# Attention scores of two heads in the two halves of the array's rows, queries and keys as single loads

## The chip, the cores and the metric

The kernel runs on one core of a Trainium2 chip. The metric is device time in microseconds of one execution, the median of several runs. The engines are PE (TensorE, matmuls), DVE (VectorE), ACT (ScalarE), POOL (GpSimd) and SP (SyncE, which issues transfers). Lines such as L745 are lines of the kernel before.

## What is computed

One layer of an encoder over 2048 tokens of width 1024, float32 in and out. The token grid is 32 rows of 64 columns.

```
h = rms_norm(x, norm1_g);  proj = h @ w_in
hy_in, q, k, v, pool_in = split(proj)              # 768, 512, 512, 512, 256 columns
y_hy   = hyena_mixer(hy_in, ...)                   # FFT convolution: irfft(rfft(z) * rfft(filter))
y_na   = neighbourhood_attention(q, k, v, rpb)     # 8 heads of 64; each token sees 8 x 16 neighbours
y_pool = pool_mixer(pool_in, ...)
x = x + concat(rms_norm of each of the three) @ w_out
x = x + expert_choice_moe(rms_norm(x), ...)        # 16 experts, 256 tokens each
out = rms_norm(x, final_g)

neighbourhood_attention, per head:
    s = (q / 8) . k_neighbours + rpb[row offset, column offset];  p = softmax(s);  out = p . v_neighbours
```

## The kernel before

The stages follow each other: `proj` (projections, with the filter's and Hyena's spectra and the pooling between them), `attention`, `out_proj`, `top_tokens`, `experts`. A scheduler that runs at build time sets the order of the instructions on each engine from the program's order and a simulated timeline; semaphores come from the tiles' uses. A tile's tag with `bufs=n` has n buffers, and the n+1st use waits for the first one's readers.

Numbers are carried as a high and a low part in the matmul type float32r. The split of the product is high x high + high x low + low x high, three terms. `mm3` (L219) issues three matmuls for it.

**Projections.** `slab` (L293) makes 128 columns of `proj` for 512 tokens. For queries (s of 3 and 4) it writes the high part to `QHd` from ACT and the low part to `QLd` from POOL (L323 to L325), for keys (s of 5 and 6) the two parts to the two halves of `KD` (L330, L331). On the host, `_layouts` (L154) puts the weight columns of a pair of heads in an order in which the dimensions of the two heads alternate, so that one partition's row of a load holds both heads.

**Filter and Hyena.** `filt` (L339) computes the filter's spectrum in 8 groups of four and writes each with one transfer to `Hd` (L413). Its `mm3` at L390 works on 64-row slices, the forward filter in the upper and the backward one in the lower half of the rows. `hyena` (L423) loads a group of `Hd` from SP (L479), and L490 multiplies it with the spectrum of z by four products of 64 partitions x 512 for each half group.

**Attention.** There are 16 units (hg, rb, g): two groups of four heads, four blocks of 8 grid rows, and g = 0 for the two outer column blocks of 16, g = 1 for the two inner ones. They are numbered 0 to 15 in this order. `load(u)` (L665) and `load_values(u)` are put in the program one unit ahead, at the beginning of unit u - 1. `load` fetches the keys of the row block (at g = 0; two transfers on SP, L680; what the block before already holds is copied by POOL), the queries (three transfers of 64 partitions, L685: the high part into both halves of the tile at_q1, from SP and from POOL, and the low part into the upper half of at_q2, from SP; the lower half of at_q2 was filled with zeros once, L653) and the bias tables (`load_bias`, L626: one tile per column block, reloaded for every row block but the third, parts from slot 4 on from POOL and the others from SP, L638). The value tiles of g = 1 are loaded once per group of heads, 1 MB each from SP (L705).

For each head the keys of high and low part lie one below the other in 128 rows, so L745 gives high x high + high x low and L746 adds low x high. L750 (DVE) adds the bias and takes the minimum, L753 (ACT) the exponential, L758 (PE) transposes it into a bank tp, L762 or L764 (DVE or ACT in turn) copies it out, and for every second head L772 (PE) multiplies with the values into a bank o, the two heads in the two halves of the array's columns. The PSUM banks of this stage are s=3, tp=3, o=2 (L1291). `load_wo` splits the weights of the output projection between the units, and `mix` (L822) prepares the first chunk of `out_proj` near the end of attention; its sums use a bank s.

## Time and profile before

| | |
|---|---|
| median of 3 runs | 3381.33 us (3378.48 to 3384.32) |
| profiled execution | 3379.93 us |
| its span | 3377.7 us |
| mean granted clock of PE | 0.973 |
| PE busy | 3222.4 us, 95% |
| DVE busy | 1919.4 us, 57% |
| ACT busy | 1519.5 us, 45% |
| POOL busy | 375.0 us, 11% |
| moved by DMA | 681.30 MB, mean 202 GB/s |

The span is the time from the first to the last instruction of the profiled execution. Busy shares are means over stages with different limits: the chain of work that ended last, followed back from the last instruction, says what set the end, and the table by stage says where. A granted clock of 1.00 is 2.4 GHz and 0.50 is 1.2 GHz; a stretch with both shows a mean. A PE piece in the chain lasts from its start to the next one's start, so pieces can be added up; the "mean ns of one" of a matmul includes its way through the array and overlaps with its neighbours.

### The profile page before, as it was taken

The page shows a single profiled execution, that of the slowest core. Times are in us where ns is not written, and L with a number is a line of the kernel's source. Part 1 is how long each engine was busy: PE and PEld are TensorE (multiplying, and loading weights), DVE is VectorE, ACT ScalarE, POOL GpSimd, SP SyncE. Part 2 cuts the span into 40 slices and gives each one's busy share as a digit, 9 for nine tenths or more (in the row PEclk, how much of TensorE's full clock was granted, in tenths as well). Part 3 has the DMA queues.
Part 4 walks back from the last instruction along what each step waited for, and adds up shares of the span by engine and source line. Part 5 has one row for each costly group of instructions (what it writes and reads, how often), then busy time and mean ns, then how long its engine had stood idle before and what let it go on. Part 6 is the DMA issues. An engine that isn't in the chain of part 4 may idle for free.

```text
span 3377.7 us, 44794 instructions
## 1 busy us (share of the span) xinstructions
PE 3222.4 (95%) x17874; PEld 2710.8 (80%) x17874; DVE 1919.4 (57%) x2571; ACT 1519.5 (45%) x2004; POOL 375.0 (11%) x492
## 2 busy tenths in 40 slices
PE   8999999687999499999999999999999999999998
PEld 6888897465788388888888888888888888888886
DVE  5124557354677665665656656556566565565665
ACT  4134422254533254554544545445445454454554
POOL 2211212222211000000000000000000000000011
PEclk9999999797999699999999999999999999999999
DMA  6675686877554356576665666666657666566586
GB/s 220 214 247 184 217 279 225 196 184 167 161 168 164 115 187 200 198 205 198 199 204 195 211 199 200 202 199 194 204 192 208 202 197 206 193 212 200 195 296 231
DMA packets 425221, 681.30 MB, mean 202 GB/s; under 512 B 28258, under 2 KB 325970, under 8 KB 424630
## 3 DMA queue, kind: packets, MB, share of 16 engines
q1 hardware_dynamic: 365414, 525.45, 49.1%
q0 software_dynamic: 31728, 111.39, 11.7%
q10 hardware_dynamic: 27872, 41.61, 3.5%
q8 instruction: 140, 2.29, 0.3%
q14 instruction: 67, 0.55, 0.0%
HBM read 573.86 MB, written 114.83 MB: 204 GB/s over the span
## 4 chain that ended last, share of the span: by engine, by line
PE 89%; DMA 7%; issue 2%; DVE 2%; ACT 1%; SPq 0%; POOL 0%; POOLq 0%; DVEq 0%; ACTq 0%
PE mm L1141 27%; PE mm L1143 14%; PE mm L221 13%; PE mm L223 13%; PE mm L222 13%; PE o L772 2%; DMA at_t<-Ce 1%; PE tp L758 1%; DMA at_q<-QLd 1%; PE tp L1110 1%; DMA Bd<-t 1%; DMA mo_xg<-Hr,mo_ix 1%; DMA mx_q<-Rd 1%; PE s L745 1%; DMA at_vw<-Vc 0%
## 5 line engine op out<-in xcount | busy, mean ns | idle before, releaser
L1141 PE MATMUL mm<-mo_xx,mo_wh 128*128 128x512 f32 x4096 | 1443.1, 397 | 0.6 <-DVE mo_xx L217 0.6
L217 DVE TENSOR_TENSOR mo_wl<-mo_raw,mo_wh 128x2048 fp32r<-128x2048 f32 x384 | 879.8, 2291 | 784.3 <-ACT mo_wh L216 784.2
L1143 PE MATMUL mm<-mo_xx,mo_wl 128*128 128x256 f32 x4096 | 1150.8, 281 | 0.0
L216 ACT ACTIVATE mo_wh<-mo_raw 128x2048 fp32r<-128x2048 f32 x384 | 735.3, 1915 | 702.2 <-issue 324.6
L1141 PEld LDWEIGHTS mm<-mo_xx,mo_wh 128*128 128x128 f32 x4096 | 769.6, 188 | 183.7 <-DVE mo_xx L217 1.0
L1143 PEld LDWEIGHTS mm<-mo_xx,mo_wl 128*128 128x128 f32 x4096 | 774.3, 189 | 0.7
L222 PE MATMUL mm<-mo_wl,mo_hh 128*128 128x512 f32 x1024 | 398.5, 389 | 0.0
L221 PE MATMUL mm<-mo_wh,mo_hh 128*128 128x512 f32 x1024 | 398.1, 389 | 0.0
L223 PE MATMUL mm<-mo_wh,mo_hl 128*128 128x512 f32 x1024 | 396.1, 389 | 0.0
L223 PEld LDWEIGHTS mm<-mo_wh,mo_hl 128*128 128x128 f32 x1024 | 192.2, 188 | 40.0
L221 PEld LDWEIGHTS mm<-mo_wh,mo_hh 128*128 128x128 f32 x1024 | 192.2, 188 | 39.9
L222 PEld LDWEIGHTS mm<-mo_wl,mo_hh 128*128 128x128 f32 x1024 | 192.2, 188 | 39.6
L1174 POOL DMA_INDIRECT Acc<-mo_y,mo_ix x30 | 69.0, 2301 | 1392.2 <-ACT mo_y L1173 1275.3
L221 PE MATMUL mm<-hT_h,w_h 128*128 128x512 f32 x512 | 205.3, 403 | 2.1 <-ACT hT_h L216 1.7
L222 PE MATMUL mm<-hT_l,w_h 128*128 128x512 f32 x512 | 207.1, 404 | 0.0
L223 PE MATMUL mm<-hT_h,w_l 128*128 128x512 f32 x512 | 206.3, 403 | 0.0
L1149 ACT ACTIVATE mo_s<-mo_s 128x512 f32<-128x512 f32 x128 | 81.0, 633 | 237.1 <-DVE mo_s L1146 237.1
L1146 DVE TENSOR_TENSOR mo_s<-mo_s,mm 128x512 f32<-128x512 f32 x256 | 174.1, 680 | 0.0
L1145 ACT ACTIVATE mo_s<-mm 128x512 f32<-128x512 f32 x256 | 147.7, 577 | 0.0
L750 DVE CUSTOM_DVE_ANT_1 at_s<-s,at_t 128x360 f32<-128x360 f32 (+5 forms) x128 | 66.9, 537 | 94.5 <-DMA at_t<-Ce 59.4
L221 PEld LDWEIGHTS mm<-hT_h,w_h 128*128 128x128 f32 x512 | 96.9, 190 | 26.1 <-ACT hT_h L216 2.4
L222 PEld LDWEIGHTS mm<-hT_l,w_h 128*128 128x128 f32 x512 | 96.8, 189 | 25.5 <-issue 3.1
(306 smaller groups left out, 3772.2 us busy)
## 6 DMA issues: line engine op xcount, KB each, us to landing
mo_raw<-in_w_gate SPq DMA_DIRECT2D x128, 1024.0 KB
mo_raw<-in_w_up SPq DMA_DIRECT2D x128, 1024.0 KB
mo_raw<-in_w_down SPq DMA_DIRECT2D x128, 1024.0 KB
w_r<-c_w_in_t SPq DMA_DIRECT2D x40, 512.0 KB
x<-in_x SPq DMA_DIRECT2D x16, 512.0 KB
Ud<-e ACTq DMA_DIRECT2D x32, 256.0 KB
wo_x<-in_x SPq DMA_DIRECT2D x16, 512.0 KB
Acc<-wo_x POOLq DMA_DIRECT2D x16, 512.0 KB, 4.2
```

The source lines that it names most:

```text
L216: self.nc.scalar.activation(hi, src, AF.Copy)
L217: self.nc.vector.tensor_tensor(lo, src, hi.bitcast(F), op=OP.subtract)
L221: mm(out, lhsT=lh, rhs=rh, start=start, stop=False)
L222: mm(out, lhsT=lh, rhs=rl, start=False, stop=False)
L223: mm(out, lhsT=ll, rhs=rh, start=False, stop=stop)
L772: nc.tensor.matmul(po[hh % 2 * 64:hh % 2 * 64 + 64, h // 2, :], lhsT=v[0:n * nkc, ci, hh * 64:hh * 64 + 64], rhs=pp[0:n * nkc, ci, :], sta ...
L1141: nc.tensor.matmul(pt[:, m].rearrange("p k t -> p (k t)"), lhsT=w[:, d, ms], rhs=xx[:, d].rearrange("p k t -> p (k t)"), start=d == 0, sto ...
L1143: nc.tensor.matmul(pt[:, m, 1], lhsT=wlo[:, d, ms], rhs=xx[:, d, 0], start=False, stop=d == 7)
L1145: nc.scalar.activation(a, pt[:, :, 1], AF.Copy)
L1146: nc.vector.tensor_tensor(a, a, pt[:, :, 0], op=OP.add)
L1149: nc.scalar.activation(s, s, AF.Silu)
L1174: nc.gpsimd.indirect_dma_start(out=self.Acc, out_offset=off, in_=y, in_offset=None, compute_op=OP.add)
```

## The change

The weight columns of queries and keys are no longer reordered on the host. Queries go to one tensor `QD` in which a partition holds high and low part of all four heads in 4 KB, and are loaded with one transfer over 128 partitions into a tile at_q. Keys go to `KD` with the two parts as columns, and are loaded with one transfer. A partition's rows are those of one head of a pair: the first head in partitions 0 to 63, the second in 64 to 127. For a pair, six matmuls of 64 rows (high x high, low key x high query, high key x low query, for each of the two heads in turn) write to two neighbouring banks of one tile `pair`. The banks become s=2 pairs, tp=2, o=2; the sums of `mix` in attention take a bank o. All tables but those of unit 0 are loaded from SP. The second half of a value tile of g = 1 comes from POOL. In the filter the real and the imaginary part of a group are each written to `Hd` twice, into both halves of the partitions, in four transfers; Hyena loads both tiles, and forms its products with one operation on 128 partitions and two on 64 in place of four on 64.

The diff, without the blank lines and the declarations:

```
@@ -171,11 +171,7 @@
     h[:, 18:24] = a["hy_short_b"][0].reshape(6, 128).T
     h[:, 24:26] = a["hy_skip"][0].reshape(2, 128).T
-    w = a["w_in"][0].reshape(2, 4, 128, 10, 256).copy()
-    qk = w[:, :, :, 3:7].reshape(2, 4, 128, 4, 2, 2, 64)
-    w[:, :, :, 3:7] = qk.swapaxes(5, 6).reshape(2, 4, 128, 4, 256)
-    w = np.ascontiguousarray(w.transpose(3, 0, 2, 1, 4))
+    w = np.ascontiguousarray(a["w_in"][0].reshape(2, 4, 128, 10, 256).transpose(3, 0, 2, 1, 4))
     rpb = a["na_rpb"][0][:, ::-1, ::-1].reshape(2, 4, 15, 31).transpose(0, 2, 1, 3)
     return {"par_f": f, "par_p": g, "par_h": h, "w_in_t": w, "rpb_r": np.ascontiguousarray(rpb).reshape(120, 31)}
@@ -320,15 +316,15 @@
             for k, b in enumerate(self.QB):
                 nc.vector.scalar_tensor_tensor(ql[:, k], pv[:, b], -0.125, qh[:, k].bitcast(F),
                                                op0=OP.mult, op1=OP.subtract)
-            for eng, dst, src in ((nc.scalar, self.QHd, qh), (nc.gpsimd, self.QLd, ql)):
-                eng.dma_start(dst[s - 3, chunk, :, m].rearrange("g p n -> p g n").bitcast(F),
+            for eng, part, src in ((nc.scalar, 0, qh), (nc.gpsimd, 1, ql)):
+                eng.dma_start(self.QD[s - 3, chunk, :, :, part, m].rearrange("g p n -> p g n").bitcast(F),
                               src.rearrange("p (g b) r c -> p g (b r c)", g=2).bitcast(F))
         elif s in (5, 6):
             kh = self.sb(pool, [128, 512], "e2", R, bufs=4)
             kl = self.sb(pool, [128, 512], "e2", R, bufs=4)
             self.split(kh, kl, pt)
-            nc.scalar.dma_start(self.KD[s - 5, m, 0:128, tok].bitcast(F), kh.bitcast(F))
-            nc.gpsimd.dma_start(self.KD[s - 5, m, 128:256, tok].bitcast(F), kl.bitcast(F))
+            nc.scalar.dma_start(self.KD[s - 5, :, 0, m, tok].bitcast(F), kh.bitcast(F))
+            nc.gpsimd.dma_start(self.KD[s - 5, :, 1, m, tok].bitcast(F), kl.bitcast(F))
         else:
             ev = self.sb(pool, [128, 512], "e2", bufs=4)
             nc.scalar.activation(ev, pt, AF.Copy)
@@ -410,7 +406,9 @@
                     k, x = g2 * 2 + e, 0 if g4 + g2 + e else 1
                     self.mm3(ph[:, e, :], self.d2p[:, 0, x], self.d2p[:, 1, x], ah[:, k, :], at[:, k, :], True, True)
                 nc.scalar.activation(ht[:, g2 * 2:g2 * 2 + 2, :], ph, AF.Copy)
-            nc.scalar.dma_start(self.Hd[g4], ht)
+            for q in range(4):
+                nc.scalar.dma_start(self.Hd[g4, q // 2, q % 2 * 64:q % 2 * 64 + 64], ht[q // 2 * 64:q // 2 * 64 + 64])
             yield
     def to_groups(self, ev, dst, a, n0, pa):
@@ -474,9 +472,9 @@
             gr = slice(g4 * 4, g4 * 4 + 4)
             at = t4([128, 4, 256])
             nc.gpsimd.dma_start(at, self.Zd[gr].rearrange("g p n -> p g n"))
-            hf = t4([128, 4, 256])
-            nc.sync.dma_start(hf, self.Hd[g4])
+            h1, h2 = t4([128, 4, 256]), t4([128, 4, 256])
+            nc.sync.dma_start(h1, self.Hd[g4, 0])
+            nc.sync.dma_start(h2, self.Hd[g4, 1])
             for g2 in range(2):
                 gs = slice(g2 * 2, g2 * 2 + 2)
                 first = [g4 * 4 + g2 * 2 + e == 0 for e in range(2)]
@@ -485,14 +483,15 @@
                     k, x = g2 * 2 + e, 2 if first[e] else 0
                     nc.tensor.matmul(pz[:, e, :], lhsT=self.d2[:, x], rhs=at[:, k, :], start=True, stop=True)
                 y, y1 = t2(), t2()
-                re, im = slice(0, 64), slice(64, 128)
-                for o, zp, hp in ((y[re], re, re), (y[im], re, im), (y1[re], im, im), (y1[im], im, re)):
-                    nc.vector.tensor_tensor(o, pz[zp], hf[hp, gs], op=OP.mult)
+                nc.vector.tensor_tensor(y, pz, h1[:, gs], op=OP.mult)
+                for q in range(2):
+                    i0, o0 = slice(q * 64, q * 64 + 64), slice(64 - q * 64, 128 - q * 64)
+                    nc.vector.tensor_tensor(y1[o0], pz[i0], h2[i0, gs], op=OP.mult)
                 if first[0]:
+                    nc.vector.tensor_tensor(y[64:65, 0], pz[64:65, 0], h2[64:65, 0], op=OP.mult)
                     nc.vector.memset(y1[0:1, 0], 0.0)
-                    nc.vector.memset(y[64:65, 0], 0.0)
-                    nc.vector.tensor_tensor(y1[64:65, 0], pz[64:65, 0], hf[64:65, 0], op=OP.mult)
+                    nc.vector.memset(y1[64:65, 0], 0.0)
                 nc.vector.scalar_tensor_tensor(y, y1, self.sign, y, op0=OP.mult, op1=OP.add)
                 pb = self.bank("tp", (128, 2, 256))
                 for e in range(2):
@@ -623,7 +622,7 @@
                               bass.AP(tensor=src.tensor, offset=src.offset, ap=[[4 * nk, 8], [60 * nk, 32], [1, 32 * nk]]))
             yield
-    def load_bias(self, tb, hg, rb, cb):
+    def load_bias(self, tb, hg, rb, cb, both):
         k = (0, 1, 1, 2)[cb]
@@ -634,7 +633,7 @@
         parts = (((0, 4, 0, 1, 4, 0, 0, 11), (4, 4, 4, 0, 4, 1, 0, 15)), ((0, 4, 4, 0, 0, 1, 0, 15),), (),
                  ((5, 3, 5, 1, 7, 0, 3, 12),))[rb]
         for q0, n, v, vs, a, as_, d, nr in parts:
-            eng = self.nc.gpsimd if q0 >= 4 else self.nc.sync
+            eng = self.nc.gpsimd if both and q0 >= 4 else self.nc.sync
             eng.dma_start(
                 tb[q0 * 16:(q0 + n) * 16, d * row:(d + nr) * row],
                 bass.AP(tensor=src.tensor, offset=src.offset + (v * 32 + hg) * 22 * row + a * row,
@@ -647,10 +646,6 @@
         units = [(hg, rb, g) for hg in range(2) for rb in range(4) for g in range(2)]
         pool = None
         bias, keys, wide, step = {}, [None], {}, 0
-        low = [kb([128, 4, 256], f"at_q2{k}", R) for k in range(2)]
-        for q in low:
-            nc.gpsimd.memset(q[64:128].bitcast(F), 0.0)
         def chunks_of(rb, wide):
             nkr, nkc = self.RB[rb][2], 32 if wide else 24
@@ -664,6 +659,7 @@
         def load(u):
             hg, rb, g = units[u]
             _, k0, nkr = self.RB[rb]
             k = None
@@ -676,19 +672,15 @@
                     have = (p0 + pn - k0) * 64
                     nc.gpsimd.tensor_copy(k[:, :, 0:have], keys[0][:, :, (k0 - p0) * 64:pn * 64])
                 keys[0] = k
-                for m in range(2):
-                    nc.sync.dma_start(k[:, m * 2:m * 2 + 2, have:nkr * 64].bitcast(F),
-                                      self.KD[hg, m].rearrange("(p x) t -> p x t", x=2)[:, :, k0 * 64 + have:(k0 + nkr) * 64].bitcast(F))
-            q1 = kb([128, 4, 256], "at_q1", R, 2)
-            q2 = low[u % 2]
-            for eng, q, d in ((nc.sync, q1[0:64], self.QHd), (nc.gpsimd, q1[64:128], self.QHd), (nc.sync, q2[0:64], self.QLd)):
-                eng.dma_start(q.rearrange("p (m x) n -> p m (x n)", x=2).bitcast(F),
-                              d[hg, rb, g].rearrange("m (p x) n -> p m (x n)", x=2).bitcast(F))
+                nc.sync.dma_start(k[:, :, have:nkr * 64].bitcast(F),
+                                  self.KD[hg].rearrange("p k m t -> p (k m) t")[:, :, k0 * 64 + have:(k0 + nkr) * 64].bitcast(F))
+            q = kb([128, 2, 2, 256], "at_q", R, 2)
+            nc.sync.dma_start(q.bitcast(F), self.QD[hg, rb, g].bitcast(F))
             for cb in (1,) if g else (0, 3):
                 if rb == 0:
                     bias[cb] = kb([128, 60 * self.CB[cb][2]], f"at_t{cb}")
-                self.load_bias(bias[cb], hg, rb, cb)
-            return k, q1, q2
+                self.load_bias(bias[cb], hg, rb, cb, u == 0)
+            return k, q
         def load_values(u):
             hg, rb, g = units[u]
@@ -702,7 +694,8 @@
                 if g:
                     if rb == 0:
                         wide[cb] = kb([128, 8, 256], f"at_vw{cb}")
-                        nc.sync.dma_start(wide[cb], values(0, 8, 128))
+                        nc.sync.dma_start(wide[cb][:, 0:4], values(0, 4, 128))
+                        nc.gpsimd.dma_start(wide[cb][:, 4:8], values(512, 4, 128))
                     v = wide[cb][:, k0 // 4:min(k0 // 4 + 4, 8)]
                 else:
                     v = kb([128, 3, 256], "at_v", F, 2)
@@ -716,7 +709,7 @@
         pool = get_pool()
         mark = nc.cur_bb.bb.instructions[-1]
         for u, (hg, rb, g) in enumerate(units):
-            (k, q1, q2), vs = ahead
+            (k, q), vs = ahead
             if g == 0:
                 kst = k
                 o = sb([128, 2, 8, 64], "at_o", F, 2)
@@ -739,11 +732,15 @@
                 po = self.bank("o", (128, 2, 128))
                 qs = slice(j * 128, j * 128 + 128)
                 for h in range(4):
-                    ps = self.bank("s")
-                    kv = kst[:, h, 0:nkr * 64].rearrange("p (r c) -> p r c", c=64)[:, :, kc0:kc0 + nkc]
-                    out = ps[:, 0:nk]
-                    nc.tensor.matmul(out, lhsT=q1[:, h, qs], rhs=kv, start=True, stop=False)
-                    nc.tensor.matmul(out, lhsT=q2[:, h, qs], rhs=kv, start=False, stop=True)
+                    if h % 2 == 0:
+                        pair = self.bank("s", (128, 2, 512))
+                        for n, (kp, qp) in enumerate(((0, 0), (1, 0), (0, 1))):
+                            for x in range(2):
+                                xs = slice(x * 64, x * 64 + 64)
+                                kv = kst[xs, kp * 2 + h // 2, 0:nkr * 64].rearrange("p (r c) -> p r c", c=64)[:, :, kc0:kc0 + nkc]
+                                nc.tensor.matmul(pair[:, x, 0:nk], lhsT=q[xs, qp, h // 2, qs], rhs=kv, start=n == 0, stop=n == 2)
+                    out = pair[:, h % 2, 0:nk]
                     s = sb([128, 480], "at_s", F, 5)
                     grid = lambda x: x.rearrange("p (r c) -> p r c", c=nkc)
                     tv = tabs[min(cb, 1) if g else cb][:, first:first + 4 * nk].rearrange("p (r h c) -> p r h c", h=4, c=nkc)[:, ::-1, h, ::-1]
@@ -819,14 +816,14 @@
                     queue.append((raw, d, ns))
             yield
-    def mix(self, pool, chunk, bufs=1):
+    def mix(self, pool, chunk, bank, bufs=1):
         nc = self.nc
         sb = lambda shape, tag, dt=F, bufs=bufs: self.sb(pool, shape, tag, dt, bufs)
         mh = sb([128, 8, 256], "mx_h", R)
         ml = sb([128, 8, 256], "mx_l", R)
         tok = slice(chunk * 256, chunk * 256 + 256)
-        pss = self.bank("s")
+        pss = bank
         for gi, (src, c, n) in enumerate(self.mixers):
             total = None
             for k in range(0, n, 2):
@@ -907,7 +904,7 @@
         for chunk in range(8):
             mh, ml, rg = ready
             if chunk < 7:
-                ready = self.mix(pool, chunk + 1, 2)
+                ready = self.mix(pool, chunk + 1, self.bank("s"), 2)
             xh = sb([128, 8, 256], "wo_hh", R, 2)
             xl = sb([128, 8, 256], "wo_hl", R, 2)
             rs = {}
@@ -1210,11 +1207,11 @@
             self.Vd = dt("Vd", [L, 512])
             self.Vc = [dt(f"Vc{k}", [32, cb[2], 512]) for k, cb in enumerate(self.CB)]
-            self.QHd, self.QLd = [dt(n, [2, 4, 2, 2, 128, 256], R) for n in ("QHd", "QLd")]
-            self.KD = dt("KD", [2, 2, 256, L], R)
+            self.QD = dt("QD", [2, 4, 2, 128, 2, 2, 256], R)
+            self.KD = dt("KD", [2, 128, 2, 2, L], R)
             self.Fd, self.Zd, self.Bd = [dt(n, [32, 128, 256]) for n in ("Fd", "Zd", "Bd")]
-            self.Hd = dt("Hd", [8, 128, 4, 256])
+            self.Hd = dt("Hd", [8, 2, 128, 4, 256])
             self.Yhd, self.Ypd = [dt(n, [256, L]) for n in ("Yhd", "Ypd")]
             self.Yad = dt("Yad", [512, L])
             self.Rd = dt("Rd", [8, L])
@@ -1288,7 +1285,7 @@
                         kpool = sbuf("attnk", right)
             psa.release()
             psf.release()
-            psa = psum("psum_b", s=3, tp=3, o=2)
+            psa = psum("psum_b", s=2, tp=2, o=2)
             pools = {}
             def left_pools():
@@ -1309,7 +1306,7 @@
                         if n % 6 == 0:
                             steps(wo, 1)
                         if n == 108:
-                            ready = self.mix(pools["early"], 0)
+                            ready = self.mix(pools["early"], 0, self.bank("o", (128, 2, 128))[:, 0])
             steps(wo)
             psa.release()
             kpool.release()
```

## Rows read from the trace of the kernel before

**Rows 1.** The page: the chain of work that ended last, by engine

```profile
PE 89%; DMA 7%; issue 2%; DVE 2%; ACT 1%; SPq 0%; POOL 0%; POOLq 0%; DVEq 0%; ACTq 0%
```

**Rows 2.** Table by stage, attention: stretch, length, busy per engine, PEclk, DMA share, GB/s

```profile
621.00:649.00 28.00, 8.78 (x32) 6.75 (x32) 4.29 (x20) 5.34 (x20) 6.16 (x8) 0.56 1.05 170
...
695.00:763.00 68.00, 62.39 (x498) 45.63 (x497) 38.58 (x121) 41.48 (x127) 21.62 (x33) 0.95 0.78 188
763.00:825.00 62.00, 39.89 (x262) 28.17 (x258) 21.77 (x77) 24.07 (x82) 12.06 (x19) 0.78 0.78 175
825.00:900.00 75.00, 72.15 (x556) 53.07 (x556) 46.73 (x138) 49.30 (x145) 23.46 (x41) 0.95 0.53 136
```

**Rows 3.** The chain in a full stretch: start us, us, what

```profile
702.51 0.22 PE s L745
...
705.75 1.02 PE o L772 x14
706.76 0.58 PE tp L758 x4
707.35 0.17 PE s L745
707.52 0.16 PE s L746
707.69 0.36 PE o L772 x2
```

**Rows 4.** The chain in the hollow stretches

```profile
631.15 17.48 DMA at_q<-QLd
...
800.82 22.41 DMA at_t<-Ce
```

**Rows 5.** Groups by shape, 649 to 896 us: busy, mean ns, idle

```profile
L745 PE MATMUL s<-at_k,at_q 128*128 128x480 f32 x32 | 16.5, 517 | 17.7 <-DVE at_min L750 17.7
...
L762 DVE COPY at_p<-tp 128x384 f32<-128x384 f32 x24 | 13.4, 556 | 18.4 <-PE tp L758 17.6 <-PE o L772 0.8
```

**Rows 6.** The chain in the filter stage, 64-row matmuls and what follows

```profile
90.54 0.42 PE fl L221
90.96 0.22 PE fl L222
...
91.41 0.22 PE fl L221 x2
...
92.07 1.06 PE tp L399 x4
...
99.79 0.86 PE tp L399 x4
```

**Rows 7.** Timeline of PE there: start us, us to the last one's end

```profile
90.47 0.49 PE L221 MATMUL fl<-f_wh,f_hh 64*128 64x256 f32 x1
...
91.03 0.60 PE L221 MATMUL fl<-f_wh,f_hh 64*128 64x256 f32 x2
```

**Rows 8.** Transfers issued, 600 to 930 us: count, KB each, median us to landing

```profile
at_q<-QLd SPq DMA_DIRECT2D x16, 256.0 KB
...
at_t<-Ce POOLq DMA_DIRECT2D x4, 360.0 KB, 18.0
...
at_t<-Ce POOLq DMA_DIRECT2D x2, 480.0 KB, 16.9
```

**Rows 9.** Table by stage, one microsecond with a single table in flight

```profile
690.00:691.00 1.00, 0.00 (x0) 0.00 (x0) 0.00 (x0) 0.00 (x0) 0.00 (x0) 0.50 0.27 106
```

**Rows 10.** Waits, 600 to 900 us: us in total, times, longest

```profile
DVE at_p L762 <- PE tp L758: 42.2, 42, 1.9
```

**Rows 11.** Hyena's products (L490): ns min/median/max, first and last start us, forms

```profile
L490 DVE TENSOR_TENSOR t<-fl,t x64: 672/689/696, 451.6 to 540.8; 64x512 f32<-64x512 f32 x64
```

**Rows 12.** Table by stage, the stretch of Hyena's products

```profile
440.00:480.00 40.00, 39.47 (x285) 37.39 (x284) 25.95 (x38) 9.89 (x15) 5.63 (x8) 1.00 0.71 227
480.00:510.00 30.00, 29.32 (x128) 23.56 (x126) 23.35 (x34) 5.90 (x10) 6.39 (x12) 1.00 1.00 365
```

89 lines of the change are left out of this document (43 added, 46 removed).

## Prediction

> **What bounds the kernel now.** The page's chain of work that ended last comes first: PE (TensorE) is 89% of it, DMA 7% [rows 1]. That is a mean over the whole kernel, so next comes the table by stage over the attention, 621 to 900 us [rows 2]. It falls into two kinds of stretch. From 695 to 763 and from 825 to 900 us PE is busy 92% and 96% of the time at a granted clock of 0.95. From 621 to 649 and 763 to 825 us (and, much like them, 669 to 695) it is busy 31% and 64%, the clock stands at 0.56 and 0.78 (a mean of 2.4 and 1.2 GHz), and DMA is 78% to 105% busy.
>
> Third, the chain in order of time. In a full stretch every piece starts where the one before ends, and all are PE: scores (L745, L746), transposes (L758), value products (L772) [rows 3]. What is added to PE there is added to the end. In the hollow stretches the chain runs through loads: four pieces of 17 to 24 us, two of queries (at_q) and two of bias tables (at_t), the first and last of which stand in [rows 4]. So the change is priced twice: its PE time where PE is the chain, its transfers where loads are.
>
> **The scores before.** A head takes two matmuls over all 128 rows. The pieces give 0.17 and 0.16 us at 360 columns and 0.22 at 480 [rows 3], that is columns/2400 plus 0.018 us. By shape (264, 288, 352 and 384 columns with 16 heads each; 360 and 480 with 32 each, the last of them in [rows 5]) this is 2 x (16 x (0.128 + 0.138 + 0.165 + 0.178) + 32 x (0.168 + 0.218)) = 44.2 us. A score block behind transposes pays no switch: its first piece is as short as its second [rows 3].
>
> **The scores after.** A pair of heads takes six matmuls of 64 rows, three per half, instead of four of 128. The kernel already has such matmuls: the filter multiplies 64-row slices by 256 columns (L221 to L223 on tile fl), first in one half alone, then in both [rows 6, 7]. Three things are read there.
> - A half alone needs 0.22 us per matmul of 256 columns. 256/2400 is 0.107, so 0.113 us per matmul is not hidden; that fits a weight load that waits for its own half.
> - With both halves in flight two matmuls pass in the same 0.22 us, and the second ends 0.11 us late (two take 0.60 us where one lasts 0.49). The halves do run side by side, but with each half's overhead in the open.
> - Going in costs 0.2 us (the first piece is 0.42), and so does going out: four transposes take 1.06 us behind the block and 0.86 elsewhere.
>
> One step of a pair thus costs 0.113 + columns/2400: 0.223, 0.233, 0.260, 0.273 us for the shapes with 8 pairs each, 0.263 and 0.313 for those with 16. That is 17.1 us, three steps 51.4. Per pair 0.2 us going in and 0.11 for the late half: 64 x 0.31 = 19.8. Together 71.2 us, 27.0 more than before. Going out I take at nothing, because a value product follows most score blocks and pays a switch already (two take 0.36 us, fourteen 1.02 [rows 3]: 0.25 us plus 0.055 each); where a transpose follows, 0.2 us comes on top, at most 64 x 0.2 = 12.8.
>
> The Trainium skill (TensorEngine Tiling (Array Packing), Key Properties) says that a change of tiling mode drains the engine, and that different tiles can load weights and multiply in parallel. The rows agree with the first. By the second a step would be about columns/2400 alone, 0.107 us where the trace shows 0.22; I go by the trace and keep the page's result as a rival.
>
> **What of it lies on the path.** 40 of the 64 pairs (units 3 to 7 and 11 to 15) run in the full stretches: 40/64 x 27.0 = 16.9 us, all exposed. The other 24 run between loads. A query load waits for the scores, a table load for the bias sums of the unit two back, so a longer unit delays those, but not loads that are late for want of bandwidth; I take half of 10.1 us, 5.1, between 0 and 10.1.
>
> **Transfers.** 48 query loads of 256 KB (three lines like the first of [rows 8]) become 16 of 512 KB, 256 KB less per unit. In the hollow stretches 170 to 175 GB/s move [rows 2], so that is 1.5 us per unit, 6 for the four units ahead of a table wait, and SP's queue gets two issues fewer in every g=0 unit (a query and a key load). I take 5 us for each of the two stretches, bounds 0 and 10. Against it: load_bias puts on SP's queue what POOL's carried for all units but unit 0, among it, at the second group of heads, two of the four parts of 360 KB and one of the two of 480 KB [rows 8]. With one table alone in flight the DMA share is 0.27 and 106 GB/s move [rows 9], so a table uses a quarter of the engines. If SP's tables share one quarter, unit 1's moved 480 KB adds 4.5 us, and units 8 and 9's 360 + 360 + 480 KB add 11.3; if they spread, nothing. Behind a table on SP that waits for the bias sums stand the values and the next queries; these waited there before for the other half of the same table. Gain and cost are of one size and I set their sum at 0, from -10 to +16. The values split over SP and POOL move the same bytes, as do the keys in one load: in that sum.
>
> **PSUM.** s goes from three single banks to two pairs, four heads ahead instead of three: no cost. tp goes from 3 to 2. Copies wait for transposes (42.2 us, 42 times [rows 10]), not the reverse, and a copy takes 0.556 us [rows 5] where a head's transposes and half a pair's value products take PE 0.58 + 0.51 [rows 3]: 0, up to +6 where other work stands ahead of the copy. The normaliser's sums (mix) borrow a bank of o while the other serves: 0, up to 1.
>
> **Filter and Hyena.** The filter writes each group in four pieces with three more issues on ACT, 1 MB instead of 512 KB: ACT is not in the chain there. In hyena 16 x 4 products become 16 x 3, 16 x 0.689 = 11.0 us less on VectorE [rows 11], against 4 MB more to load where DMA is already 71% to 100% busy; PE is 98% busy there with projections [rows 12], so neither moves the end at first order. If Hyena ended earlier, the first attention loads, which need its memory, would too: -6; if the transfers delay it, +5. I take 0. POOL's filling of zeros goes, and the weight columns are rearranged on the host, outside the program: 0.
>
> **Sum.** 16.9 + 5.1 + 0 + 0 + 0 = +22.0 us on the profiled execution's 3379.9: 3401.9. The median of the runs, 3381.3, is 1.4 above that execution, so 3403 us.
>
> **Rivals.**
> - *The six matmuls pack better (faster).* Place: the score block. If a half's weight load hides behind the other half's matmul and the switch is free, three passes replace four, 33.1 us instead of 44.2; 52/64 of the 11.1 count (40 pairs and half of 24): -9, so 3372, and 3356 with the good ends of transfers and Hyena (-10, -6). It decides from 44.2/64 = 0.69 us per pair downwards. The Trainium skill (same page, Theoretical Speedup) gives up to twice for 64 rows. Against it: the measured steps [rows 6].
> - *Loads give it back (no change).* -10 and -6: 3403 - 16 = 3387. For it: the loads in the chain [rows 4]. Against it: few bytes are saved and the slow tables stay.
> - *The tables on SP lengthen the waits (slower still).* The two table waits grow by 4.5 and 11.3: 3403 + 16 = 3419, and with going out on 52/64 of the pairs (10.4) 3429. For it: [rows 4, 9].
> - *The halves don't overlap (the change doesn't do what it says).* Six steps one by one, or other work put between: 102.8 + 12.8 - 44.2 = 71.4, 52/64 of it 58: 3439. Against it: [rows 7].
>
> **How the numbers follow.** Forecast 0.55 (3392 to 3414), packing 0.11, no change 0.15, tables 0.16, no overlap 0.03. A measurement of this kernel tells some 0.2% (6.8 us) from no change. Faster is nearly the packing case, 0.10; same is the no-change case and the forecast's low edge, 0.18; slower 0.72. The range leaves out most of the packing case, the far end of the tables and no overlap: 3377 to 3428.
>
> **What would show it.** Right: blocks of six on 64 rows, 1.0 to 1.25 us per pair in the full stretches, the first piece 0.2 us longer; attention some 22 us longer and every stage behind it as long as now. Wrong: blocks under 0.7 us; hollow stretches that shrink or grow by over 10 us; or projections that end elsewhere than at 608 us.

## The result, and the profile after

The change made the kernel faster: 3353.66 us (median of 4 runs, 3349.01 to 3357.59) against 3382.82 for the kernel before beside it, a ratio of 0.9914 (95% interval 0.9897 to 0.9932), some 29 us. 3403 was forecast, and a range from 3377 to 3428. The profiled execution took 3349.01 us, its span 3347.2, at a mean granted clock of 0.976. One execution of a later run, a_hyena_old, took 4875.21 us at a mean granted clock of 0.604; it is the one of that run with a trace, and it counts in no ratio.

In the kernel after, the scores stand on L742, bias sums on L747, exponentials on L750, transposes on L755, their copies on L759 and L761, value products on L769, the query load on L678 and the tables on L637; the helper `mm3` is L217 to L219. In runs with added lines these numbers shift by a few.

The table by stage (columns as in [rows 2]), over stretches with about the same work: units 0 to 2 (hollow), 4 to 7 (full) and 8 to 10 (hollow). First before, then after:

```profile
628.00:693.00 65.00, 39.82 (x227) 27.49 (x225) 18.05 (x71) 21.25 (x72) 7.88 (x11) 0.74 0.92 179
708.00:756.00 48.00, 46.07 (x385) 34.13 (x386) 28.98 (x97) 31.49 (x97) 18.00 (x29) 1.00 0.83 207
756.00:823.00 67.00, 42.34 (x288) 30.31 (x282) 22.10 (x77) 25.33 (x84) 12.89 (x20) 0.80 0.83 181
```

```profile
622.00:672.00 50.00, 42.39 (x259) 27.31 (x259) 19.72 (x76) 22.83 (x74) 9.81 (x14) 0.67 0.79 197
686.00:742.00 56.00, 49.93 (x422) 34.09 (x420) 31.17 (x100) 35.96 (x106) 13.52 (x21) 0.93 0.70 195
742.00:789.00 47.00, 41.10 (x311) 27.03 (x312) 22.07 (x80) 25.78 (x82) 13.88 (x21) 0.87 0.74 202
```

The hollow stretches became shorter, by 15 and 20 us; PE was busy 61% and 63% of them before and is busy 85% and 87% after. The full stretch between them became longer, by 8 us, with PE busy 96% before and 89% after and a granted clock of 0.93 in place of 1.00. The last full stretch, from the first bias sum of unit 11 to the last of unit 15, takes 65.3 us before and 63.8 after.

The chain in order of time, score blocks and what stands beside them (start us, us, what):

```profile
683.15 0.69 PE s L742 x6
683.84 1.02 PE o L769 x14
684.86 0.58 PE tp L755 x4
...
702.18 0.86 PE s L742 x6
...
708.47 0.59 PE s L742 x6
```

A block is six matmuls for two heads. It takes 0.69 us at 360 columns, 0.86 at 480 and 0.59 at 288. The kernel before took two times 0.33 at 360 [rows 3], and four times columns/2400 + 0.018 = 0.87 at 480. So the scores cost what they did. Taken apart: 0.69 = 3 x (360/2400 + 0.018) + 0.186; 0.86 = 3 x 0.218 + 0.206; 0.59 = 3 x 0.138 + 0.176. A step of a pair is as short as a matmul of 128 rows, and about 0.19 us goes for going in. (The three sizes alone don't part the step from going in; the timeline of a_halves_apart below does, with a step of 0.16 us at 360 columns.) The value products behind the block take 1.02 us for fourteen, as before [rows 3]: going out costs nothing more.

Where the chain of before ran through loads [rows 4], the chain of after does so (start us, us, what):

```profile
590.75 6.94 DMA Yhd<-hy_x
597.71 24.59 DMA at_v<-Vc
622.32 17.60 DMA at_t<-Ce
...
653.53 18.75 DMA at_t<-Ce
...
721.85 12.99 DMA wo_raw<-in_w_out
...
771.03 17.96 DMA at_t<-Ce
```

No wait for a query load to land stands in it any more. The wait for the second group's table ended at 800.82 + 22.41 = 823.2 us before [rows 4] and ends at 771.03 + 17.96 = 789.0 now, 34.2 us earlier; the span is 30.5 us shorter. So the gain lies ahead of 789 us, and some 4 us are given back behind. Its first part is seen in the key loads, first of before, then of after (ns of the issue min/median/max, time of the first and the last issue):

```profile
L680 SPq DMA_DIRECT2D at_k<-KD x16: 528/602/8893, 604.5 to 836.7; - x16
```

```profile
L675 SPq DMA_DIRECT2D at_k<-KD x8: 552/579/8292, 591.4 to 796.0; - x8
```

The first of them comes 13.1 us earlier, and the remaining 21 us are won between that load and 789 us. That is no sum of two causes: the first bias sum of unit 0 comes only 5.0 us earlier (623.8 us instead of 628.8), and most of the gain shows in the two hollow stretches. The waits of the bias sums, 600 to 900 us (in total, times, longest), before and after:

```profile
DVE at_s L750 <- DMA at_t<-Ce: 59.4, 6, 17.2
...
DVE at_s L750 <- PE tp L758: 1.2, 1, 1.2
```

```profile
DVE at_s L747 <- PE tp L755: 37.0, 28, 6.0
...
DVE at_s L747 <- DMA at_t<-Ce: 18.3, 4, 9.4
...
PE tp L755 <- DVE at_p L759: 1.8, 1, 1.8
```

41 us of waiting for tables went, and 36 us of waiting for transposes came. The second is new, and it was not in the forecast. These are waits of DVE, which is not the bottleneck. What PE waited for in the same stretch, before and after:

```profile
PE s L745 <- DMA at_q<-QHd: 33.8, 4, 11.5
PE s L745 <- DVE at_min L750: 20.9, 5, 9.8
...
PE s L746 <- DMA at_q<-QLd: 8.0, 5, 4.8
...
PE o L772 <- ACT at_p L764: 3.7, 1, 3.7
```

```profile
PE s L742 <- DMA at_q<-QD: 10.5, 2, 6.0
...
PE s L742 <- DVE at_min L747: 9.0, 1, 9.0
...
PE o L769 <- DVE at_p L759: 8.4, 10, 3.2
...
PE o L769 <- ACT at_p L761: 7.0, 6, 5.4
```

The waits for queries fell from 41.8 to 10.5 us and those of scores for bias sums from 20.9 to 9.0; those of value products for the copies rose from 3.7 to 15.4.

### The profile page after: what moved, and what is told of

The parts are those of the page before. It is cut to its first block, busy times and chain, and to the rows that moved or that the text cites. A ratio compares the mean times of both kernels' runs of the same rounds, so it can differ in the third digit from the quotient of the medians.

```text
span 3347.2 us, 45004 instructions
## 1 busy us (share of the span) xinstructions
PE 3225.9 (96%) x18002; PEld 2702.0 (81%) x18002; DVE 1905.3 (57%) x2555; ACT 1525.1 (46%) x2004; POOL 361.7 (11%) x468
## 4 chain that ended last, share of the span: by engine, by line
PE 89%; DMA 6%; issue 2%; DVE 2%; ACT 1%; SPq 0%; POOL 0%; ACTq 0%; POOLq 0%; DVEq 0%
PE mm L1138 27%; PE mm L1140 14%; PE mm L217 13%; PE mm L218 13%; PE mm L219 13%; PE o L769 2%; DMA at_t<-Ce 2%; PE tp L755 1%; PE tp L1107 1%; PE s L742 1%; DMA at_v<-Vc 1%; DMA mo_xg<-Hr,mo_ix 1%; PE tp L395 0%; PE tp L1079 0%; PE fl L484 0%
## 5 line engine op out<-in xcount | busy, mean ns | idle before, releaser
L217 PE MATMUL mm<-mo_wh,mo_hh 128*128 128x512 f32 x1024 | 398.1, 389 | 0.0
L219 PE MATMUL mm<-mo_wh,mo_hl 128*128 128x512 f32 x1024 | 396.1, 389 | 0.0
L217 PEld LDWEIGHTS mm<-mo_wh,mo_hh 128*128 128x128 f32 x1024 | 192.2, 188 | 40.1
L219 PEld LDWEIGHTS mm<-mo_wh,mo_hl 128*128 128x128 f32 x1024 | 192.2, 188 | 39.9
L217 PE MATMUL mm<-hT_h,w_h 128*128 128x512 f32 x512 | 206.3, 406 | 2.1 <-ACT hT_h L212 2.1
L219 PE MATMUL mm<-hT_h,w_l 128*128 128x512 f32 x512 | 204.8, 400 | 0.0
L217 PEld LDWEIGHTS mm<-hT_h,w_h 128*128 128x128 f32 x512 | 96.9, 190 | 26.1 <-ACT hT_h L212 2.8
L219 PEld LDWEIGHTS mm<-hT_h,w_l 128*128 128x128 f32 x512 | 96.6, 189 | 23.5 <-issue 1.3
## 6 DMA issues: line engine op xcount, KB each, us to landing
x<-in_x SPq DMA_DIRECT2D x16, 512.0 KB, 10.5
```

What stands on the lines that cost most here:

```text
L217: mm(out, lhsT=lh, rhs=rh, start=start, stop=False)
L219: mm(out, lhsT=ll, rhs=rh, start=False, stop=stop)
```

## The experiments

Ratios are to the kernel before in the same series, with a 95% interval; the kernel after stands at 0.9914. 0.0010 of a ratio is 3.4 us, and a difference of two ratios of four or five runs each carries some 8 us of uncertainty. A trace is of one execution.

**The score block.** Theory: the forecast's 0.113 us per step, read from the filter, is no price of 64 rows but of the filter's stationary columns, which lie 16 elements (64 bytes) apart; attention's are contiguous. Rival: the price is real and the order of the halves hides it.

Three matmuls of the first head, then three of the second:

```
-for n, (kp, qp) in enumerate(((0, 0), (1, 0), (0, 1))):
-    for x in range(2):
+for x in range(2):
+    for n, (kp, qp) in enumerate(((0, 0), (1, 0), (0, 1))):
```

> The changed kernel with the six score matmuls of a pair in another order: three of the first head, then three of the second. If the halves overlap because alternating instructions let one half load weights and multiply while the other does, a block at 360 columns goes from 0.68 us to 1.2 to 1.6 us (one half alone: 0.113 + 0.150 per matmul, six of them 1.58), and the time goes up by 20 to 45 us. If PE starts the second half's matmuls while the first half's still run whatever the order, a block stays under 0.9 us and the time within 10 us.

Measured: 3358.57 us, 0.9935 [0.9918, 0.9951]; the interval overlaps that of the kernel after. The chain:

```profile
686.26 0.69 PE s L742 x6
686.96 1.02 PE o L769 x14
```

and PE's timeline, cut off after 0.27, 0.40 and 0.60 us of the same block (start us, us to the last one's end, ... count):

```profile
686.19 0.44 PE L742 MATMUL s<-at_k,at_q 64*128 64x360 f32 x2
686.19 0.60 PE L742 MATMUL s<-at_k,at_q 64*128 64x360 f32 x4
686.19 0.76 PE L742 MATMUL s<-at_k,at_q 64*128 64x360 f32 x6
```

The six start in pairs, two every 0.16 us, although three of one half were issued ahead of the other three. The scheduler did not put them back: in the compiled program PE's instructions stand in the edited order in all 64 blocks. The halves run beside each other in either order, and the rival falls.

The filter's columns laid contiguous:

```
-hh, hl = sb([128, L], "f_hh", R), sb([128, L], "f_hl", R)
+hh, hl = sb([128, 16, 128], "f_hh", R), sb([128, 16, 128], "f_hl", R)
-self.split(hh[:, bs], hl[:, bs], h2)
+ab = slice(b * 32, b * 32 + 32)
+self.split(hh[:, :, ab], hl[:, :, ab], h2.rearrange("p (a b) -> p b a", b=16))
-hh, hl = [v.rearrange("p (a b) -> p b a", b=16) for v in (hh, hl)]
```

> The changed kernel with the filter's stationary operand laid out without gaps: the hidden states are written in the order in which the 64-row matmuls read their 128 columns, instead of read with a step of 16 elements. The result is the same. Theory A (the 0.22 us per 64-row matmul of 256 columns is a weight load that nothing hides in row tiles): pieces stay at 0.22 us alone and 0.22 for two. Theory B (it is a slow weight load because its columns lie 64 bytes apart; dense weights hide): pieces fall to 0.11 to 0.13 us, as in the score blocks, where 3 steps of 360 columns take 0.68 us with the switch.

Measured: 3347.63 us in a single run, beside 3381.04 for the kernel before. The chain there, which answers to [rows 6]:

```profile
89.07 0.31 PE fl L217
89.38 0.12 PE fl L218
89.50 0.12 PE fl L219
89.62 0.12 PE fl L217 x2
89.74 0.12 PE fl L218 x2
89.86 0.12 PE fl L219 x2
```

A matmul of 64 rows and 256 columns takes 0.12 us, 256/2400 + 0.013, where it took 0.22, and two in both halves take the same 0.12. By form, in the stretch from 60 to 150 us, the weight loads of the kernel after and of this one (busy, mean ns of one, idle):

```profile
L219 PEld LDWEIGHTS fl<-f_wh,f_hl 64*128 64x128 f32 x23 | 6.2, 313 | 0.0
```

```profile
L219 PEld LDWEIGHTS fl<-f_wh,f_hl 64*128 64x128 f32 x24 | 3.5, 186 | 0.0
```

The layout of the columns alone makes the difference: the theory holds.

The Trainium skill (TensorEngine Tiling (Array Packing), Key Properties) says that a change of mode drains the engine and that different tiles load weights and multiply in parallel. This case's blocks agree with both: 0.18 to 0.21 us going in, and steps without an open weight load. Its "Up to 2×" for 64 rows (Theoretical Speedup) could not come here: in the kernel before three of the four halves of rows of a head's two matmuls held data, so the most to be won was four matmuls becoming three. Three steps and the switch, 0.69 us, stand where four matmuls took 0.66.

**Filter and Hyena.** Theory: the shorter Hyena lets attention's memory, and so its loads, start earlier. Rival: PE sets the end of the stage, and nothing comes of it. The old forms of L413, L479 and L490 were put back into the kernel after, and the new ones into the kernel before (the lines of the diff above from @@ -410 to @@ -485, and the shape of `Hd`).

> The changed kernel with filter and Hyena as before: one write of a group to Hd, one load, four products of 64 partitions. Attention stays changed. If the 12 us that Hyena ends earlier (keys first issued at 591 instead of 604 us) go through to the end: +10 to +14 us, 3364 to 3368, with the first key load at 602 to 606 us. If the earlier start is eaten up by the bandwidth of the first hollow stretch: under +5 us.

Measured: 0.9970 [0.9959, 0.9981], so 0.0056 or 19 us slower than the kernel after, where 10 to 14 were expected.

> The kernel before with only filter and Hyena changed (two loads of a group, three products). Undoing this part of the changed kernel cost 15 us. If an earlier start of attention is worth as much with the old transfers: 10 to 15 us faster than before, 3366 to 3371, the first key load at 590 to 594 us instead of 604. If the old transfers are bound by bandwidth and eat it: within 5 us of before, with the first key load early all the same.

Measured: 3365.22 us, 0.9961 [0.9947, 0.9975]: 13 us faster than the kernel before. Its key loads (as above) begin 9.7 us earlier than those of before, a little later than expected:

```profile
L683 SPq DMA_DIRECT2D at_k<-KD x16: 536/602/6995, 594.8 to 818.4; - x16
```

This part works by itself, on either kernel. In this trace the first bias sum of unit 0 comes 5.5 us earlier than in that of before and the last one of unit 15 comes 19.8 us earlier (868.9 instead of 888.7 us): what the earlier loads give is won on the way through the hollow stretches, not at the start. The projections' last matmul ends at 607 to 611 us in all three kernels, so the rival is right on the end of the projections, and it does not matter: attention's loads follow Hyena. In the kernel before, Hyena's last result is sent off from SP at 603.8 us and the first key load is issued behind it at 604.5; in the kernel after these are 590.8 and 591.4. The values of after start where that result has landed (590.75 + 6.94 in the chain above). Whether the keys wait for the memory or for their place on SP's queue behind that result is not told apart.

**The transfers.** Theory: fewer and larger query transfers let the table behind them land earlier. Rivals: it is the queue that the tables are on, or the values' second queue.

Tables back on both queues (`u == 0` to `True`), and the values in one transfer on SP:

> The changed kernel with the table parts from slot 4 on issued from POOL in all units, as before. My prediction's step: tables on SP share a quarter of the engines and lengthen the waits, so this one would be faster by 5 to 16 us, 3338 to 3349. Rival: tables queued on SP behind the queries land in the order in which they are needed, and POOL's compete with the queries: slower by 3 to 15 us. Third: within 3 us.

> The changed kernel with the value tiles of g=1 as one transfer of 1 MB each from SP. If the halves on POOL relieve SP's queue (2 MB before unit 1 and again before unit 9): slower by 4 to 15 us, 3358 to 3369, most of it between units 1 and 3 and between 9 and 11. If only the bytes count: within 3 us.

Measured: 0.9924 [0.9908, 0.9941] and 0.9926 [0.9910, 0.9943]. Both intervals hold the kernel after: neither move (3 and 4 us slower by the ratios) is clear of the noise, and a gain of 5 to 16 us from tables on both queues, the forecast's step, is not seen.

A first undoing of the query load added a third transfer into a tile that nothing read, alone and together with all other old transfers:

```
-nc.sync.dma_start(q.bitcast(F), self.QD[hg, rb, g].bitcast(F))
+nc.sync.dma_start(q[0:64].bitcast(F), self.QD[hg, rb, g, 0:64].bitcast(F))
+nc.gpsimd.dma_start(q[64:128].bitcast(F), self.QD[hg, rb, g, 64:128].bitcast(F))
+spare = kb([128, 1024], "at_sp", F, 2)
+nc.sync.dma_start(spare[0:64], self.QD[hg, rb, g, 0:64].rearrange("p k m n -> p (k m n)").bitcast(F))
```

> The changed kernel with only the queries in three transfers of 64 partitions and 256 KB (two from SP, one from POOL; the third is read by nothing). All transfers of attention in the old form cost 24 us. If the queries carry most of that (256 KB more per unit, two more issues per unit, and half the partitions per transfer): +12 to +24 us, 3366 to 3378, with both hollow stretches (48.6 and 46.2 us between the first bias sums of units 0 and 3, 8 and 11) longer by 6 to 12 us each. If it is the other transfers: within 6 us of 3354.

> The changed kernel with attention's transfers as before: queries in three transfers of 64 partitions and 256 KB each (two from SP, one from POOL; the third goes to a tile that nothing reads), keys in two, tables from slot 4 on from POOL, values of g=1 whole from SP. Scores, PSUM banks, filter and Hyena stay changed. Theory 1 (the transfers shorten the two hollow stretches, 15.5 us from unit 0's first bias sum to unit 3's and 21.3 us from unit 8's to unit 11's in the trace): those come back to 60 to 68 us each and the time goes up by 25 to 40 us, 3380 to 3393. Theory 2 (the paired scores with four heads ahead shorten them): the stretches stay at 46 to 50 us and the time within 5 us of 3354. Theory 3 (Hyena's earlier end is what helps, by loads that start in a quiet time): the time goes up by under 10 us.

Measured: 1.0024 [1.0014, 1.0035] and 0.9992 [0.9981, 1.0003]. Nothing had to wait for the third transfer, so it ran ahead of its unit. In the next runs the additional bytes go into the tile of the queries, which is waited for. That changed little (1.0012 and 1.0002 below): the running ahead was not what cost.

Two transfers of 64 partitions, from SP and POOL, or both from SP; then one of 128 partitions and 256 KB more on all 128; then the three of 64 partitions; then these three with tables, values and keys in the old form too:

```
+nc.sync.dma_start(q[0:64].bitcast(F), self.QD[hg, rb, g, 0:64].bitcast(F))
+nc.gpsimd.dma_start(q[64:128].bitcast(F), self.QD[hg, rb, g, 64:128].bitcast(F))   # a_q_two_sp: nc.sync
```

```
+nc.sync.dma_start(q[:, 0:2].bitcast(F), self.QD[hg, rb, g].bitcast(F))             # a_q_more
+nc.sync.dma_start(q[:, 2].bitcast(F), self.QD[hg, rb, g, :, 0].bitcast(F))
```

```
+q = kb([128, 4, 2, 256], "at_q", R, 2)                                             # a_q_three_waiting
+(the two transfers of a_q_two into q[:, 0:2])
+nc.sync.dma_start(q[0:64, 2:4].bitcast(F), self.QD[hg, rb, g, 0:64].bitcast(F))
```

> The changed kernel with the queries in two transfers of 64 partitions and 256 KB, one from SP and one from POOL: the same bytes. If what the single load buys is its one issue and all partitions at once: +4 to +12 us, 3358 to 3366. If the bytes of the third transfer were what mattered: within 3 us of 3354.

> The changed kernel with the queries in two transfers of 64 partitions, both from SP. With the second one from POOL it took 11 us more than with one load. If the split itself costs (one more issue per unit, each over half the partitions): 3361 to 3368 again. If it was POOL's queue, where the second half stands behind transfers that wait for other work: within 4 us of 3354.

> The changed kernel with the whole query load and a second transfer of 256 KB over all 128 partitions from SP, which nothing reads and which waits for the scores as the first does. If bytes and issues count, as the third transfer of 64 partitions did with 20 us: 3366 to 3378, and the waits of the bias sums for at_t up from 18 us to 30 to 40. If only transfers of 64 partitions hurt: within 5 us of 3354.

> As the run with queries in three transfers, but the third one, which nothing reads, goes into the same tile as the other two and so waits for the scores as they do. In the earlier run it waited for nothing, ran ahead on SP's queue (four of them in a row at 669 us) and held a table back to 684 us, which may be what made it 33 us slower. If that was it: +3 to +12 us here, 3357 to 3366. If three transfers and 768 KB per unit cost 24 us and more by themselves: 3378 and above.

> The changed kernel with all transfers of attention in the old form, the third query transfer waiting for the scores. What is left of the change is then scores and PSUM banks, and filter and Hyena; the kernel before with filter and Hyena changed took 3365. If the transfers are worth the 11 us between that and 3354: 3362 to 3369. If the scores and banks are: 3352 to 3357.

The last two columns are of the trace: the time from the first bias sum of unit 0 to that of unit 3 and from unit 8's to unit 11's, together, and how much of it PE was not busy. In the kernel after they are 94.8 and 12.1 us, in the kernel before 131.6 and 49.7.

| query loads | ratio | above the kernel after | hollow, us | PE not busy, us |
|---|---|---|---|---|
| two halves, SP and POOL | 0.9949 [0.9933, 0.9966] | 12 us | 115.8 | 26.6 |
| two halves, SP | 0.9951 [0.9934, 0.9968] | 13 us | 108.7 | 20.0 |
| one, and 256 KB more | 0.9953 [0.9939, 0.9967] | 13 us | 109.5 | 23.3 |
| three of 64 partitions | 1.0012 [1.0002, 1.0022] | 33 us | 125.2 | 34.4 |
| three, and all other transfers old | 1.0002 [0.9992, 1.0012] | 30 us | 120.9 | 31.2 |

The waits of the bias sums for tables, with two halves (SP and POOL), with three transfers, and with all transfers old, beside the 18.3 us of the kernel after:

```profile
DVE at_s L748 <- DMA at_t<-Ce: 31.9, 4, 11.7
```

```profile
DVE at_s L749 <- DMA at_t<-Ce: 40.7, 4, 15.5
```

```profile
DVE at_s L749 <- DMA at_t<-Ce: 19.5, 3, 12.5
```

The query load in one piece is what the transfers bring, some 30 us: undoing the other transfers too adds nothing. The cost of cutting it up lies in the hollow stretches, where PE stands longer. That it works through the table behind the queries, as the theory has it, is not shown: the table waits grow with two and three transfers, but with all transfers old they are no longer than in the kernel after, and the kernel is as slow. Splitting the same bytes costs 12 us, wherever the second half is issued. What of the rest is bytes, number of transfers or the 64 partitions each of them fills is not told apart: 256 KB more over all partitions cost as much as the split with none more.

**The banks.** Theory: tp of 2 instead of 3 costs; rival: the packed blocks do. The kernel before with s=4, tp=2, o=2:

> The kernel before with the PSUM banks of attention divided as s=4, tp=2, o=2 in place of 3, 3, 2: four scores ahead, two transposes. In the changed kernel the full stretches grew by 9 us (units 4 to 7) and 4 us (units 12 to 15). If two tp banks make that: +6 to +14 us, 3387 to 3395, with units 4 to 7 at 52 to 57 us instead of 47.4. If not: within 4 us of before.

Measured: 1.0015 [1.0005, 1.0026], 5 us slower, just under the 6 to 14 expected. The kernel after with `psum("psum_b", s=2, tp=3, o=1)`:

> The changed kernel with PSUM banks of attention divided as two pairs, tp=3 and o=1. Two banks for transposes cost the kernel before 6 us, units 4 and 12 there 2.2 to 2.4 us each. If they cost the same here and one bank o is enough (the copy of o, 0.37 us, is all that the next value products wait for, 32 times): 0 to 6 us faster, 3348 to 3354, with units 4 and 12 at 10.3 to 11 us. If one bank o costs more than tp gains: 3357 to 3372.

Measured: 0.9899 [0.9883, 0.9916], 5 us under the kernel after, with overlapping intervals. With all transfers in the old form, tp=2 stands at 1.0002 (above), and the kernel before with the new Hyena at 0.9961. The same with tp=3, o=1:

> All transfers of attention in the old form (three query transfers of 64 partitions, tables on both queues, values and keys as before), the packed scores kept, and the banks s=2 pairs, tp=3, o=1 instead of tp=2, o=2. The same kernel with tp=2, o=2 stood at 1.0002 of the kernel before (about 3381.5 us), and the kernel before with the new filter and Hyena at 0.9961 (about 3365). If that difference of some 14 us is the banks of the transposes, this run is at 0.9961 to 0.998 (3365 to 3372). If it is the packed scores themselves (their switch, or the coarser blocks of two heads), it stays at 0.9995 to 1.001 (3379 to 3384).

Measured: 3369.89 us, 0.9961 [0.9946, 0.9977]. At three banks tp the packed scores cost nothing, to some 7 us, against single heads under like transfers (0.9961 and 0.9961), and the 0.0041 or 14 us are the banks, tp and o together. With the new transfers the same banks are worth 5 us. The waits of the bias sums for transposes, in the kernel before with tp=2, with all transfers old and tp=2, and with these and tp=3:

```profile
DVE at_s L750 <- PE tp L758: 32.0, 33, 3.3
```

```profile
DVE at_s L749 <- PE tp L757: 48.9, 30, 8.1
```

```profile
DVE at_s L749 <- PE tp L757: 4.6, 6, 2.4
```

With two banks the transposes fall behind, at_s (five buffers) fills, and the next bias sum waits: three pairs of traces show that. That this wait is the price is not shown. In the kernel after with tp=3, o=1 the bias sums wait so:

```profile
DVE at_s L747 <- DMA at_t<-Ce: 41.4, 4, 13.1
...
DVE at_s L747 <- PE tp L755: 8.8, 9, 3.1
```

28 us of waiting for transposes went and 23 of waiting for tables came, and the kernel is 5 us faster. On PE's side the transposes wait for the copies to empty a bank only 1.8 us in the kernel after, where I looked for the price; the value products wait for the copies 15.4 us instead of 3.7. From the first bias sum of unit 4 to that of unit 8 the kernel before takes 47.4 us and 59.0 with tp=2, the kernel after 56.7 and 49.6 with tp=3, o=1; so the full stretch that became longer is a place where the banks tell. With old transfers it is 54.5 and, at a granted clock of 0.75, 53.9 us, and the traces don't place the 14 us: the profiled executions of these two kernels took 3381.3 (tp=2) and 3378.4 us (tp=3), the latter its slowest.

**What can be added.** The query load issued from POOL in the kernel after:

```
-nc.sync.dma_start(q.bitcast(F), self.QD[hg, rb, g].bitcast(F))
+nc.gpsimd.dma_start(q.bitcast(F), self.QD[hg, rb, g].bitcast(F))
```

> The changed kernel with the whole query load issued from POOL. SP's queue then carries one transfer less per unit and the tables behind it are issued earlier, while the queries stand in POOL's queue behind the weights of the output projection. If SP's queue is what holds the tables back: 3 to 10 us faster, 3344 to 3351. If POOL's order costs more: 3358 to 3370.

Measured: 0.9906 [0.9890, 0.9923], 3 us under the kernel after and inside its interval. With tp=3, o=1 and the filter's contiguous columns as well:

> The changed kernel with three edits at once: three banks for the transposes and one for the value products in the packed pairs (alone 8 us under the changed kernel), the query load issued from POOL instead of SP (alone 6 us under), and the filter's stationary columns laid contiguous (alone 6 us under in one look). If the three gains lie in different places, the time is about 3353 - 20 = 3334 us. If the first two buy the same thing (both shorten the hollow stretches, which end on the table's load), the sum is about 3353 - 8 - 6 = 3340 us; if the filter's gain was only the spread of a single look, 3340 to 3346 us.

Measured: 3331.77 us (3327.21 to 3337.31), 0.9856 [0.9834, 0.9879]: 20 us under the kernel after, 49 under the kernel before. The three together give no less than their sum (5, 3 and, from a single run, 6 us). Where each of the 20 us lies a single profile doesn't tell: the four runs of this kernel lie 10 us apart, more than each gain.

## Why the prediction was wrong

The step of the prediction that failed is the price of a score step, 0.113 us + columns/2400, taken from the filter; attention's blocks show 0.018 + columns/2400, and the +22 us that followed from it came to none. Beside it the terms for transfers and for Hyena, both set at 0, measured -30 and -13 us. The runs form a chain from the kernel before to the kernel after, each step one group of edits:

| step | ratio | us | forecast |
|---|---|---|---|
| new filter and Hyena (b_hyena_new) | 1 to 0.9961 | -13 | 0 (-6 to +5) |
| packed scores, tp=3, o=1 (a_loads_old_tp3) | to 0.9961 | 0 | +22 |
| tp=2, o=2 (a_loads_old_waiting) | to 1.0002 | +14 | 0 (up to +6) |
| new transfers (the kernel after) | to 0.9914 | -30 | 0 (-10 to +16) |
| sum | | -29 | +22 |

Each step carries some 6 us of uncertainty, and its size depends on the order: the filter and Hyena are worth 19 us in the kernel after, the banks 5 us in the kernel before and 5 with the new transfers, and the new transfers 21 us at tp=3, o=1 (0.9961 to 0.9899). The old form of the loads in the two middle rows has the number, partitions and bytes of before, not its layout in memory.

- *Scores, the step that gave the sign.* Going in was right (0.2 forecast, 0.19 measured); the 0.11 for a late half did not show. The step of 0.113 + columns/2400 was wrong: it is 0.018 + columns/2400. By pieces all blocks come to 8 x (0.574 + 0.604 + 0.684 + 0.724) + 16 x (0.694 + 0.844) = 45.3 us against 44.2 before, +1.1 instead of +27.0. The rows of the filter [rows 6] were read rightly; that they would hold for attention was not examined. Their stationary columns are 64 bytes apart, which stands in the code, and the same 0.22 us for one and for two matmuls [rows 7] left open whether the weight load is slow or unhidden. The rival "pack better" named the point of decision, 0.69 us per pair on average, and the blocks come to 45.3/64 = 0.71: no gain, and next to no loss.
- *Transfers.* The term was mis-sized: -30 where -10 was the good end. I priced the bytes saved at the rate of the stretch, 1.5 us per unit. The runs show that the split costs 12 us at equal bytes, so the bytes alone were not what to price; PE's idle time in the two hollow stretches is 31.2 us with all transfers old and 12.1 with the new ones. The opposing +4.5 and +11.3 for tables on SP [rows 8, 9] did not show: with the tables back on both queues the kernel was no faster (0.9924).
- *Filter and Hyena.* The mechanism stood in the forecast ("If Hyena ended earlier, the first attention loads, which need its memory, would too"), but was set at 0 because PE is 98% busy [rows 12]. PE's busy share bounds the projections, which did end at 608 us as forecast; Hyena's chain of products runs beside them and ended 13 us earlier. From 510 to 550 us DVE was busy 39.35 of 40 us before and 31.84 after:

```profile
510.00:550.00 40.00, 37.80 (x155) 30.36 (x156) 39.35 (x50) 15.94 (x21) 6.25 (x14) 0.96 0.59 190
```

```profile
510.00:550.00 40.00, 40.00 (x175) 32.34 (x174) 31.84 (x38) 15.11 (x19) 12.18 (x22) 1.00 0.84 300
```

  The first line was there to be read: DVE full, PE not.
- *PSUM.* Up to +6 was allowed for; 14 us were measured with the old transfers and 5 in two other kernels. I looked at who waits between transposes and copies [rows 10] and found PE free. The waits that grew lie elsewhere: those of the bias sums for transposes, two steps ahead in the chain of buffers, and those of the value products for copies. Through which of them the time is lost stays open.
- *What I said would show it wrong* did in the main: blocks of 0.69 us at 360 columns, if not under 0.7 at 480, where 1.0 to 1.25 was forecast, and hollow stretches that shrank by more than 10 us. The third sign, projections that end elsewhere than at 608, was the wrong place to look at.

## What to carry to other kernels

A duration taken from another place of the kernel carries that place's operand layout with it: before it becomes a price, compare strides, not only shapes. Packing two heads by rows saves a matmul in four and pays it back in the switch at blocks of three; its worth here lies in what the layout allows, a query load in one piece over all 128 partitions. When the next stage's loads wait for something in a stage whose engine is full, follow that, not the engine's end; and when banks change hands, look also at the waits one buffer further up, and let the time of a run, not the sum of an idle engine's waits, say what they cost.

## What was not expected of the hardware

- Stationary columns 64 bytes apart: a weight load of 64x128 lasts 313 ns in the records instead of 186, and the matmul of 256 columns takes 0.22 us instead of 0.12.
- Matmuls in the two halves of the rows start together even where three of one half are issued ahead of three of the other (0.69 us per block of 360 columns in both orders).
- Splitting a 512 KB load over 128 partitions into two over 64, at equal bytes, cost the kernel 12 us (with some 8 us of uncertainty) in 16 such loads, on one queue or on two.
